# First FFN of an encoder block: four pairs of w1/w3 feature tiles by seven half-size products

## The chip, the cores and the metric

The kernel runs on one core of one Trainium2 chip. The metric is the device time of one execution in microseconds; the time of a kernel is the median of its runs. Engines are named as in the profile: PE (TensorE matmuls), PEld (its weight loads), DVE (VectorE), ACT (ScalarE), POOL (GpSimd), SP (the queue that issues most loads).

## The reference

One layer of an encoder block over x of 512 tokens by 1024 features, in float32:

```python
x = x + 0.5 * swiglu(rms_norm(x, ffn1_norm), ffn1_w1, ffn1_w3, ffn1_w2)     # first FFN
h = rms_norm(x, mix_norm); p = h @ w_in                                     # two mixers and gates
x = x + (gate_a * y_a + gate_b * y_b) @ w_out
x = x + 0.5 * swiglu(rms_norm(x, ffn2_norm), ffn2_w1, ffn2_w3, ffn2_w2)     # second FFN
out = rms_norm(x, final_norm)

def swiglu(h, w1, w3, w2):
    return (jax.nn.silu(h @ w1) * (h @ w3)) @ w2
```

w1 and w3 are 1024 x 2816, w2 is 2816 x 1024. The change touches only the two products with w1 and w3 in the first FFN, and what they need.

## The kernel before

Everything is held with features on the 128 partitions and the 512 tokens along the free side: x is eight tiles `xT[c]` (128 x 512). A matmul takes a 128 x 128 weight tile as the stationary side and streams 512 token columns. Each float32 product is made of three matmuls of a reduced-width type (`mm3`): operands are split into a high part (a cast) and a low part (the rest), and high x high, high x low and low x high are added up in PSUM.

The 2816 hidden features are 22 tiles, j = 0 to 21. For each j the loop in `ffn` loads a 1024 x 128 slice of w1 and one of w3 (512 KB each, `load_raw`, three buffers of tag `raw`, issued on SP's queue), splits it (`split_w`: cast on ACT into `whi`, subtraction on DVE into `wlo`, two buffers each), and `nrm.cols` runs 8 k-tiles x 3 = 24 matmuls into one PSUM bank, `pa` for w1 and `pb` for w3. The x that goes in is scaled by the norm's gain but not yet by the tokens' 1/rms: `rstd` comes out of a sum over all features only during j = 1, so `hidden` multiplies both results by `rstd` on DVE (`fa`, `fb`), takes Silu on ACT, multiplies (`fh`) and splits the hidden tile for w2 (`hh`, `hl`). Tile 0 and the reading and transposing of x are interleaved by hand at the start, with each engine's order fixed by a chain (`Queued`). All else is ordered by a scheduler at compile time: it places an instruction on its engine when its inputs are ready and its buffers free, earlier in the program first. `tc.issue_after(...)` holds an instruction behind a given one on the same engine.

After the 22 tiles, `ffn` multiplies by w2 (`pd`, m = 0 to 7, 22 k-tiles each, loaded in three pieces), adds to `xT[m]`, and `mix_add` parks x and prepares the next norm. `during` is a list of side jobs at given j: `load_params` (2) and `masks` (4) and `place_params` (10), which transposes a block of parameters on PE and casts some small weights on POOL. PSUM is eight banks in three pools: `pm` 2, `pr` 3, `pf` 3.

Of the kernel before, what the change touches and what calls it, by code (L numbers as in the profile page):

```python
# [18 lines left out]
P = 128  # L19
T = 512  # L20
D = 1024
KD = D // P
DFF = 2816
KF = DFF // P
# [26 lines left out]
def kernel(  # L51
# [22 lines left out]
    def tmp(name, shape=(P, T), dt=F32, tag="t", **kw):  # L74
        return tp.tile(list(shape), dt, tag=tag, name=name, **kw)
# [30 lines left out]
    def load_raw(aps, kt, n):  # L106
        raw = wp.tile([P, kt, n], F32, tag="raw", name="raw", bufs=3)
        for c0, src in aps:
            loads.append(nc.sync.dma_start(raw[:, :, c0:c0 + src.shape[1]],
                                           src.rearrange("(k p) c -> p k c", p=P)))  # L110
        return raw

    def split_w(raw, kt, n, eng=None, hi_eng=None):
        hi = wp.tile([P, kt, n], F32R, tag="whi", name="whi", bufs=2)
        lo = wp.tile([P, kt, n], F32R, tag="wlo", name="wlo", bufs=2)
        (hi_eng or act).copy(hi[:], raw[:])  # L116
        (eng or dve).tensor_tensor(lo[:], raw[:], hi[:].bitcast(F32), op=ALU.subtract)  # L117
        return hi, lo
# [4 lines left out]
    def mm3(ps, whi, wlo, xhi, xlo, first, last):  # L123
        pe.matmul(ps, whi, xhi, start=first, stop=False)  # L124
        pe.matmul(ps, whi, xlo, start=False, stop=False)  # L125
        return pe.matmul(ps, wlo, xhi, start=False, stop=last)  # L126
# [14 lines left out]
    def split(dst_hi, dst_lo, src, hi_eng="act"):  # L141
        cast = act.copy(dst_hi, src) if hi_eng == "act" else dve.tensor_copy(dst_hi, src)
        dve.tensor_tensor(dst_lo, src, dst_hi.bitcast(F32), op=ALU.subtract)
        return cast
# [4 lines left out]

    xctx = ExitStack()  # L150
    rtp = xctx.enter_context(tc.tile_pool(name="xr1", bufs=1, side="right"))
    xT = [rtp.tile([P, T], F32, name=f"xT{c}") for c in range(KD)]

    class Norm:

# [32 lines left out]
        def add(s, c):  # L188
            s.scale(c)
            s.square(c)  # L190
# [28 lines left out]
    def pc(i):  # L219
        return par[:, i:i + 1]  # L220
# [24 lines left out]
    with tc.tile_pool(name="x0", bufs=1) as x0:  # L245
# [21 lines left out]
                qpe.transpose(xps[c][:, b * P:(b + 1) * P], xin[c][:, b, :], ident[:])  # L267

        def x_hi(c):
            nrm.hi[c] = xp.tile([P, T], F32R, tag=f"xh{c}", name=f"xh{c}")  # L270
            from_ = (xps if c < 2 else xT)[c][:]
            if c % 2:
                qact.activation(nrm.hi[c][:], from_, AF.Copy, scale=pc(PAR_FFN1 + c))
            else:
                qdve.tensor_scalar(nrm.hi[c][:], from_, pc(PAR_FFN1 + c), None, op0=ALU.mult)

        def x_lo(c):
            nrm.lo[c] = xp.tile([P, T], F32R, tag=f"xl{c}", name=f"xl{c}")
# [154 lines left out]
    def place_params():  # L433
# [9 lines left out]
        pool.tensor_copy(ux[q1], loraw[q1, :])  # L443
        pool.tensor_tensor(ux[q1], loraw[q1, :], f32(ux[q1]), op=ALU.subtract)

    def ffn(nrm, w1, w3, w2, nxt, during=(), first=None, final=None):
        with tc.tile_pool(name="hp", bufs=1) as hp:
            hh, hl = [], []
            def hidden(j, pa, pb):
# [7 lines left out]
                dve.tensor_tensor(h[:], b[:], sa[:], op=ALU.mult)  # L457
                hi = hp.tile([P, T], F32R, name=f"hh{j}")
                lo = hp.tile([P, T], F32R, name=f"hl{j}")
                split(hi[:], lo[:], h[:], "dve")  # L460
                hh.append(hi)
                hl.append(lo)

            summed = None
            for j in range(KF):
# [21 lines left out]
                hidden(j, pa, pb)  # L487
# [12 lines left out]
            if final:  # L500
                final[1](hh, hl, held)
# [713 lines left out]
```

## Time and profile before

| | |
|---|---|
| median of 3 runs | 1189.98 us (1189.31 to 1190.92) |
| the profiled execution | 1189.68 us, of which the span of instructions is 1188.0 us |
| granted TensorE clock | 0.997 of full |
| PE, DVE, ACT, POOL busy | 1173.7, 657.1, 459.3, 87.4 us |
| bytes moved by DMA | 122.52 MB |

How to read it: the profile is of one execution. The span runs from the first to the last instruction; 1.7 us of the execution lie around it. A row of the timeline is start, duration, engine, line, operation and output <- input; a row of the groups adds a count, busy time, mean duration in ns, and the idle time ahead of it with what ended it. A matmul's duration includes the time in which its results drain, so successive matmuls overlap: the distance between starts is what one costs.

### The profile page before, as it was taken

How to read it: one execution, taken by the hardware profiler on the slowest of the kernel's cores; microseconds unless marked ns; L12 is line 12 of the kernel's file. 1: busy time of each engine (PE TensorE's matmuls, PEld its weight loads, DVE VectorE, ACT ScalarE, POOL GpSimd, SP SyncE). 2: the span in 40 equal slices, each digit the busy share in tenths (PEclk: the TensorE clock that was granted, in tenths of full speed). 3: DMA queues.
4: the chain of work that ended last, by engine and by line, in shares of the span. 5: the costliest groups of instructions: out<-in, count | busy, mean ns of one | idle time of the engine just before them, and what ended most of it. 6: DMA issues, size and time to landing. Idle time of an engine off the chain costs nothing.

```text
span 1188.0 us, 15711 instructions
## 1 busy us (share of the span) xinstructions
PE 1173.7 (99%) x6264; PEld 946.0 (80%) x6264; DVE 657.1 (55%) x983; ACT 459.3 (39%) x746; POOL 87.4 (7%) x138
## 2 busy tenths in 40 slices
PE   9999999999999999999999999999999999999997
PEld 7888888888887888887777776778888888888886
DVE  6645554533434697786767656766545454534221
ACT  6322222222223764346786765424222222223222
POOL 1200000001111111411000020121000000000100
PEclk9999999999999999999999999999999999999999
DMA  6333333333334243344122243633333333325211
GB/s 179 111 106 90 106 89 106 89 93 104 114 116 112 78 120 112 109 140 116 37 64 88 81 132 115 211 92 97 89 106 89 103 93 105 91 87 161 89 36 71
DMA packets 201783, 122.52 MB, mean 103 GB/s; under 512 B 9934, under 2 KB 191246, under 8 KB 201710
## 3 DMA queue, kind: packets, MB, share of 16 engines
q1 hardware_dynamic: 195134, 107.62, 31.1%
q0 software_dynamic: 3760, 12.06, 3.2%
q10 hardware_dynamic: 2816, 1.84, 0.5%
q8 instruction: 49, 0.80, 0.3%
q14 instruction: 24, 0.20, 0.1%
HBM read 110.82 MB, written 10.68 MB: 102 GB/s over the span
## 4 chain that ended last, share of the span: by engine, by line
PE 92%; DVE 3%; ACT 3%; DMA 1%; issue 1%; SPq 0%; ACTq 0%; DVEq 0%
PE pb L126 7%; PE pa L126 7%; PE pa L125 7%; PE pb L125 7%; PE pb L124 7%; PE pa L124 7%; PE pd L126 5%; PE pd L124 5%; PE pd L125 5%; PE pgt L124 3%; PE pgt L125 2%; PE pgt L126 2%; PE pk L124 2%; PE pk L125 2%; PE pk L126 2%; PE po L124 2%
## 5 line engine op out<-in xcount | busy, mean ns | idle before, releaser
L116 ACT CAST whi<-raw 128x1024 fp32r<-128x1024 f32 (+3 forms) x193 | 192.7, 999 | 592.0 <-PE pa L125 177.8
L117 DVE TENSOR_TENSOR wlo<-raw,whi 128x1024 fp32r<-128x1024 f32 (+3 forms) x193 | 224.3, 1162 | 125.1 <-ACT whi L116 125.0
L126 PE MATMUL pb<-xh,wlo 128*128 128x512 f32 x344 | 133.9, 389 | 0.0
L126 PE MATMUL pa<-xh,wlo 128*128 128x512 f32 x344 | 133.9, 389 | 0.0
L125 PE MATMUL pa<-xl,whi 128*128 128x512 f32 x344 | 133.9, 389 | 0.0
L124 PE MATMUL pb<-xh,whi 128*128 128x512 f32 x344 | 133.9, 389 | 0.0
L125 PE MATMUL pb<-xl,whi 128*128 128x512 f32 x344 | 133.9, 389 | 0.0
L124 PE MATMUL pa<-xh,whi 128*128 128x512 f32 x344 | 133.9, 389 | 0.0
L455 DVE TENSOR_TENSOR fb<-pb,rstd 128x512 f32<-128x512 f32 x43 | 29.7, 691 | 139.5 <-PE pb L126 139.5
L126 PE MATMUL pd<-hh,wlo 128*128 128x512 f32 x264 | 104.6, 396 | 0.0
L125 PE MATMUL pd<-hl,whi 128*128 128x512 f32 x264 | 104.2, 395 | 0.0
L124 PE MATMUL pd<-hh,whi 128*128 128x512 f32 x264 | 104.2, 395 | 0.0
L126 PEld LDWEIGHTS pb<-xh,wlo 128*128 128x128 f32 x344 | 64.5, 188 | 13.7 <-DVE wlo L241 0.5
L125 PEld LDWEIGHTS pb<-xl,whi 128*128 128x128 f32 x344 | 64.6, 188 | 13.5
L124 PEld LDWEIGHTS pb<-xh,whi 128*128 128x128 f32 x344 | 64.6, 188 | 13.5
L126 PEld LDWEIGHTS pa<-xh,wlo 128*128 128x128 f32 x344 | 64.6, 188 | 13.4
L125 PEld LDWEIGHTS pa<-xl,whi 128*128 128x128 f32 x344 | 64.5, 188 | 13.5
L124 PEld LDWEIGHTS pa<-xh,whi 128*128 128x128 f32 x344 | 64.6, 188 | 13.4
L451 DVE TENSOR_TENSOR fa<-pa,rstd 128x512 f32<-128x512 f32 x43 | 29.7, 691 | 70.2 <-PE pa L126 70.2
L126 PEld LDWEIGHTS pd<-hh,wlo 128*128 128x128 f32 x264 | 49.6, 188 | 12.3 <-DVE wlo L117 0.5
L125 PEld LDWEIGHTS pd<-hl,whi 128*128 128x128 f32 x264 | 49.6, 188 | 11.9
L124 PEld LDWEIGHTS pd<-hh,whi 128*128 128x128 f32 x264 | 49.6, 188 | 11.8
(397 smaller groups left out, 2031.1 us busy)
## 6 DMA issues: line engine op xcount, KB each, us to landing
raw<-in_ffn_w_dram SPq DMA_DIRECT2D x121, 512.0 KB
raw<-in_w_in_dram SPq DMA_DIRECT2D x40, 512.0 KB
raw<-in_ffn_w_dram SPq DMA_DIRECT2D x12, 384.0 KB
raw<-in_w_out_dram SPq DMA_DIRECT2D x8, 512.0 KB
gsave<-gs SPq DMA_DIRECT2D x9, 256.0 KB
xin<-in_x_dram SPq DMA_DIRECT2D x8, 256.0 KB
xsave<-xT POOLq DMA_DIRECT2D x8, 256.0 KB, 2.3
G<-gsave POOLq DMA_DIRECT2D x8, 256.0 KB, 3.0
```

The source lines that it names most:

```text
L116: (hi_eng or act).copy(hi[:], raw[:])
L117: (eng or dve).tensor_tensor(lo[:], raw[:], hi[:].bitcast(F32), op=ALU.subtract)
L124: pe.matmul(ps, whi, xhi, start=first, stop=False)
L125: pe.matmul(ps, whi, xlo, start=False, stop=False)
L126: return pe.matmul(ps, wlo, xhi, start=False, stop=last)
L451: dve.tensor_tensor(a[:], pa[:], nrm.rstd[:], op=ALU.mult)
L455: dve.tensor_tensor(b[:], pb[:], nrm.rstd[:], op=ALU.mult)
```

## The change

For j = 6 to 13 the loop takes two feature tiles at a time (`wino`, four times: `NW, W0 = 4, 6`). The product of a pair is seen as blocks of two by two: weights by feature tile (j or j+1) and half of the 1024 inputs, tokens by half of the inputs and half of the 512 tokens. A scheme of the Strassen family makes the four result blocks out of seven products of blocks instead of eight, with sums of blocks on both sides. A product is 24 matmuls of 256 columns: w1 and w3, four k-tiles, three terms.

- The scheme needs x already normalized. `renorm` multiplies `xT` in place by gain and `rstd` (after j = 2 and 3 of the program) and splits it again into `B`. The raw x is written to memory first (`xkeep`, by POOL) and read back on SP's queue after the last j.
- `token_sums` (after j = 4 and 5) makes four sums of token blocks, split into `TB`.
- Three buffers of 8 KB a partition (tag `R`) hold x at first, the token sums, and then in turn the weight blocks of the pairs: r for the first half of the inputs (a11, a21) and r for the second (a12, a22), 1 MB each, loaded as 256 columns of w1 and w3.
- Of the four weight sums two are made on DVE (`s1`, and s1 + a11 in the place of a11), and two by transfers that POOL issues and that add to their target (`onto`): A11 onto a21, and A12 onto a11. Each `onto` is two transfers of 256 KB with rows of 512 B.
- Each of the seven weight blocks is split into high and low parts (`w_parts`); two splits in three go to the buffers of `whi` and `wlo`, the third into two of the three `raw` buffers.
- The products are p11, p2, p1, p12, p3, p4, p22, in this order on PE; seven additions or subtractions of 512 elements on DVE and one copy on ACT combine them. From j = 6 on `hidden_n` needs no `rstd`.
- For j > 1 of the first FFN the cast of the hidden tile moves from DVE to ACT; `place_params` moves from j = 10 to j = 16; the split x of the start moves to a pool `hx` whose tiles later hold hidden tiles 6 to 13.

The diff, cut to its core:

```diff
-    xT = [rtp.tile([P, T], F32, name=f"xT{c}") for c in range(KD)]
+    def place(shape, name, dt=F32):
+        return rtp.tile([P, *shape], dt, tag="R", name=name, bufs=3)
+    xr = [place((KD // 2, T), f"xr{i}") for i in range(2)]
+    xT = [xr[c // 4][:, c % 4] for c in range(KD)]
+    xkeep = dp.tile([KD, P, T], F32, name="xkeep")
...
+        for i in range(2):
+            nc.gpsimd.dma_start(xkeep[4 * i:4 * i + 4].rearrange("c p t -> p c t"), xr[i][:])
...
+            def renorm(cs):
+                for c in cs:
+                    dve.scalar_tensor_tensor(xT[c], xT[c], pc(nrm.gain + c), nrm.rstd[:], op0=ALU.mult, op1=ALU.mult)
+                    hi = xp.tile([P, T], F32R, tag=f"xh{c}", name=f"xn{c}")
+                    lo = xp.tile([P, T], F32R, tag=f"xl{c}", name=f"xm{c}")
+                    split(hi[:], lo[:], xT[c])
+                    B.append((hi, lo))
...
+            def token_sums(n):
+                l, r = slice(0, HT), slice(HT, T)
+                if n == 0:
+                    TB.append(place((2, HK, HT), "tsum"))
+                D = TB[0]
+                if n == 0:
+                    dve.tensor_tensor(D[:, 0], xr[0][:, :, r], xr[0][:, :, l], op=ALU.subtract)
+                    t_parts(0, D[:, 0])
+                    dve.tensor_tensor(D[:, 1], xr[1][:, :, r], xr[0][:, :, r], op=ALU.subtract)
+                    t_parts(1, D[:, 1])
+                else:
+                    dve.tensor_tensor(D[:, 0], xr[1][:, :, r], D[:, 0], op=ALU.subtract)
+                    t_parts(2, D[:, 0])
+                    dve.tensor_tensor(D[:, 1], D[:, 0], xr[1][:, :, l], op=ALU.subtract)
+                    t_parts(3, D[:, 1])
...
+            def w_parts(src):
+                n = count[0] % 3
+                count[0] += 1
+                hi = wp.tile([P, KD, P], F32R, tag="raw" if n == 2 else "whi", name="ah", bufs=3 if n == 2 else 2)
+                lo = wp.tile([P, KD, P], F32R, tag="raw" if n == 2 else "wlo", name="al", bufs=3 if n == 2 else 2)
+                split(hi[:], lo[:], src)
+                return hi, lo
+            def wino(j):
+                cs = slice(j * P, (j + 2) * P)
+                A = []
+                for h in range(2):
+                    r = place((2 * HK, 2 * P), "aw")
+                    for i, w in enumerate((w1, w3)):
+                        loads.append(nc.sync.dma_start(
+                            r[:, i * HK:(i + 1) * HK],
+                            w[0][h * HK * P:(h + 1) * HK * P, cs].rearrange("(k p) c -> p k c", p=P)))
+                    A.append((r[:, :, 0:P], r[:, :, P:2 * P]))
+                (a11, a21), (a12, a22) = A
+                p11 = w_parts(a11)
+                s1 = wp.tile([P, KD, P], F32, tag="raw", name="asum", bufs=3)
+                add = lambda o, x_, y_: dve.tensor_tensor(o, x_, y_, op=ALU.add)
+                add(s1[:], a22, a21)
+                def onto(dst, k0, c):
+                    for i, w in enumerate((w1, w3)):
+                        pool.dma_start(dst[:, i * HK:(i + 1) * HK],
+                                       w[0][k0 * P:(k0 + HK) * P, c * P:(c + 1) * P].rearrange("(k p) c -> p k c", p=P),
+                                       accum_op=ALU.add)
+                onto(a21, 0, j)
+                add(a11, s1[:], a11)
+                p2 = w_parts(a11)
+                p1 = w_parts(s1[:])
+                p12 = w_parts(a12)
+                onto(a11, HK, j)
+                p3 = w_parts(a21)
+                p4 = w_parts(a11)
+                p22 = w_parts(a22)
...
+                def product(name, pool_, parts, block):
+                    ps = pool_.tile([P, 2, HT], F32, tag="b", name=name)
+                    hi, lo = parts
+                    for i in range(2):
+                        for k, (bh, bl) in enumerate(block):
+                            q = i * HK + k
+                            mm3(ps[:, i], hi[:, q], lo[:, q], bh, bl, k == 0, k == HK - 1)
+                    return ps
...
+                pa = product("wa", pm, p11, x_block(0, 0))
+                t1 = half_tmp("t1")
+                act.copy(t1[:], pa[:])
+                pb = product("wb", pr, p2, t_block(2))
+                u2 = half_tmp("u2")
+                dve.tensor_tensor(u2[:], pb[:], t1[:], op=ALU.subtract)
...
+            ready = {2: lambda: renorm(range(0, HK)), 3: lambda: renorm(range(HK, KD)),
+                     4: lambda: token_sums(0), 5: lambda: token_sums(1)}
...
+                if first and j in ready:
+                    ready[j]()
+                j += 1
+            if first:
+                xr[:] = [place((KD // 2, T), f"xb{i}") for i in range(2)]
+                for i in range(2):
+                    loads.append(nc.sync.dma_start(xr[i][:], xkeep[4 * i:4 * i + 4].rearrange("c p t -> p c t")))
...
-    ffn(nrm, ffn1_w1, ffn1_w3, ffn1_w2, mix_add, {2: load_params, 4: masks, 10: place_params}, (first, second))
+    ffn(nrm, ffn1_w1, ffn1_w3, ffn1_w2, mix_add, {2: load_params, 4: masks, 16: place_params}, (first, second))
```

More of the change, by code (lines that the diff above doesn't have):

```diff
@@ L269, in x_hi @@
         def x_hi(c):
-            nrm.hi[c] = xp.tile([P, T], F32R, tag=f"xh{c}", name=f"xh{c}")
+            pair = hx.tile([P, 2, T], F32R, tag=f"h{6 + c}", name=f"px{c}")
+            nrm.hi[c], nrm.lo[c] = pair[:, 0], pair[:, 1]
             from_ = (xps if c < 2 else xT)[c][:]
@@ L277, in x_lo @@
         def x_lo(c):
-            nrm.lo[c] = xp.tile([P, T], F32R, tag=f"xl{c}", name=f"xl{c}")
             from_ = (xps if c < 2 else xT)[c][:]
@@ L448, in ffn, with hidden_parts @@
             hh, hl = [], []
+            def hidden_parts(j, h):
+                if first and W0 <= j < W0 + KD:
+                    t = hx.tile([P, 2, T], F32R, tag=f"h{j}", name=f"hid{j}")
+                else:
+                    t = hp.tile([P, 2, T], F32R, tag=f"h{j}", name=f"hid{j}")
+                split(t[:, 0], t[:, 1], h, "act" if first and j > 1 else "dve")
+                hh.append(t[:, 0])
+                hl.append(t[:, 1])
             def hidden(j, pa, pb):
@@ L457, in hidden, with hidden_n @@
                 dve.tensor_tensor(h[:], b[:], sa[:], op=ALU.mult)
[L458 to L462, printed above, removed]
-            summed = None
-            for j in range(KF):
+                hidden_parts(j, h[:])
+            def hidden_n(j, a, b, sa, h):
+                act.activation(sa, a, AF.Silu)
+                dve.tensor_tensor(h, b, sa, op=ALU.mult)
+                hidden_parts(j, h)
@@ new lines, in ffn @@
+            summed = None
+            j, normed_ = 0, False
+            ready = {2: lambda: renorm(range(0, HK)), 3: lambda: renorm(range(HK, KD)),
+                     4: lambda: token_sums(0), 5: lambda: token_sums(1)}
+            while j < KF:
+                if first and W0 <= j < W0 + 2 * NW:
+                    if not normed_:
+                        nrm.hi, nrm.lo = [h for h, l in B], [l for h, l in B]
+                        normed_ = True
+                    wino(j)
+                    j += 2
+                    continue
@@ L486, in ffn @@
                         during[j]()
-                hidden(j, pa, pb)
+                if normed_:
+                    sa, h = tmp("fs"), tmp("fh")
+                    hidden_n(j, pa[:], pb[:], sa[:], h[:])
+                else:
+                    hidden(j, pa, pb)
+                if first and j in ready:
+                    ready[j]()
+                j += 1
+            if first:
+                xr[:] = [place((KD // 2, T), f"xb{i}") for i in range(2)]
+                for i in range(2):
+                    loads.append(nc.sync.dma_start(xr[i][:], xkeep[4 * i:4 * i + 4].rearrange("c p t -> p c t")))
+                xT[:] = [xr[c // 4][:, c % 4] for c in range(KD)]
             cuts = ((0, 8), (8, 8), (16, 6))
```

35 lines of the change are left out of this document (added).

## The prediction

> **What bounds the kernel now.** I read first the page's busy times and the shares of its chain of waits.
>
> ```profile
> span 1188.0 us, 15711 instructions
> PE 1173.7 (99%) x6264; PEld 946.0 (80%) x6264; DVE 657.1 (55%) x983; ACT 459.3 (39%) x746; POOL 87.4 (7%) x138
> PE 92%; DVE 3%; ACT 3%; DMA 1%; issue 1%; SPq 0%; ACTq 0%; DVEq 0%
> ```
>
> The second line is busy time and share by engine, the third the share of the chain that ended last. TensorE is 99% busy and 92% of the chain: time taken off its stream comes off the kernel, unless something else then holds it up. So the next view is the stretch that the change rewrites. In order of time, feature tile 6 (the first that the change pairs) starts at 77.06 us and tile 14 at 164.25 us; below are these two starts, the matmul before the first, and the busy table of this stretch and of the one ahead of it (columns: stretch, length, PE, PEld, DVE, ACT, POOL with counts, clock, DMA share, GB/s).
>
> ```profile
> 76.83 0.39 PE L126 MATMUL pb<-xh,wlo 128*128 128x512 f32 x1
> 77.06 0.39 PE L124 MATMUL pa<-xh,whi 128*128 128x512 f32 x1
> 164.25 0.39 PE L124 MATMUL pa<-xh,whi 128*128 128x512 f32 x1
> 31.00:77.00 46.00, 46.00 (x204) 38.09 (x204) 26.75 (x34) 13.01 (x15) 6.12 (x7) 1.00 0.39 114
> 77.06:164.25 87.19, 87.19 (x387) 72.14 (x385) 43.90 (x58) 21.61 (x24) 0.00 (x0) 1.00 0.33 97
> ```
>
> Eight feature tiles x 2 weight matrices x 8 k-tiles x 3 terms = 384 matmuls fill 87.19 us without a hole (the three others are a transpose and the edges): 0.227 us each, at full clock. VectorE is half idle there (43.90 of 87.19), ScalarE three quarters. The groups of that stretch give the price of one:
>
> ```profile
> L124 PE MATMUL pb<-xh,whi 128*128 128x512 f32 x64 | 24.9, 389 | 0.0
> L117 DVE TENSOR_TENSOR wlo<-raw,whi 128x1024 fp32r<-128x1024 f32 x16 | 19.6, 1222 | 1.3 <-ACT whi L116 1.3
> L116 ACT CAST whi<-raw 128x1024 fp32r<-128x1024 f32 x16 | 16.9, 1054 | 65.6 <-PE pa L125 34.9 <-PE pb L125 30.7
> L126 PEld LDWEIGHTS pa<-xh,wlo 128*128 128x128 f32 x64 | 12.0, 188 | 2.6
> L457 DVE TENSOR_TENSOR fh<-fb,fs 128x512 f32<-128x512 f32 x8 | 5.5, 692 | 0.7
> ```
>
> ScalarE's 65.6 us before `whi` end on matmuls: the splits wait for a free `whi`, not for data. The weights come early and TensorE never waits for them.
>
> **The change part by part.**
>
> *TensorE.* Four pairs of tiles now take 7 products each; a product is 2 matrices x 4 k-tiles x 3 terms = 24 matmuls of 256 columns. So 4 x 168 = 672 half matmuls replace 384 whole ones, each with its own weight load. Everything hangs on the spacing of 256-column matmuls. The trace has some in the attention logits (L978, L979); two places in order of time, and their group:
>
> ```profile
> 571.17 0.19 PEld L978 LDWEIGHTS lp<-kb,qa 128*128 128x128 f32 x1 [0.65 <-ACT qrn L818]
> 571.28 0.19 PEld L979 LDWEIGHTS lp<-klc,qb 128*128 128x128 f32 x1
> ...
> 571.70 0.28 PE L979 MATMUL lp<-klc,qb 128*128 128x256 f32 x1
> 571.82 0.23 PE L980 MATMUL lp<-dmask,identb 128*128 128x128 bf16 x1
> ...
> 574.39 0.27 PE L979 MATMUL lp<-klc,qb 128*128 128x256 f32 x1
> 574.50 0.23 PE L980 MATMUL lp<-dmask,identb 128*128 128x128 bf16 x1
> L979 PE MATMUL lp<-klc,qb 128*128 128x256 f32 x8 | 2.2, 279 | 0.0
> ```
>
> After a 256-column matmul the next starts 0.12 and 0.11 us later. Two weight loads follow each other in 0.11 us, so loads (188 ns each, but overlapping) do not quite set the pace. I take 0.120 us: 672 x 0.120 = 80.6 us against 384 x 0.227 = 87.1, a gain of **6.5 us**. The rows lie one matmul deep, not in a stream; as bounds I take 0.117 (78.6 us, gain 8.5) and 0.123 (82.7 us, gain 4.4). The pair becomes 168 x 0.12 = 20.2 us, a product 2.9 us.
>
> The Trainium skill, "TensorE: Matmul & The Clock Gate", section "Back-to-back issue gap", gives N/2.4 + 2.5 ns for an isolated gap, an estimate of 109 ns at 256 columns. By it the sum would be 73 us. The trace disagrees at 512 columns already: 227 ns against its 216.
>
> *VectorE and ScalarE in the pairs.* Each product needs its weights split (cast 1.05, subtract 1.22), seven a pair where there were four; two block sums run on VectorE (1.22 each); seven combinations of 512 elements out of PSUM and four operations for the two hidden tiles (0.69 each). In one tile before, VectorE and the queue of loads look so:
>
> ```profile
> 78.06 0.69 DVE L457 TENSOR_TENSOR fh<-fb,fs 128x512 f32<-128x512 f32 x1
> 78.67 1.22 DVE L117 TENSOR_TENSOR wlo<-raw,whi 128x1024 fp32r<-128x1024 f32 x1
> 79.80 0.42 DVE L142 CAST hh<-fh 128x512 fp32r<-128x512 f32 x1
> 79.91 16.15 SPq L109 DMA_DIRECT2D raw<-in_ffn_w_dram  x4
> ```
>
> Start to start these are 0.61 (78.06 to 78.67) and 1.13 (78.67 to 79.80). VectorE: 9 x 1.13 + 11 x 0.61 = 16.9 us of a 20.2 us pair (by durations 9 x 1.22 + 11 x 0.69 = 18.6). ScalarE: 7 x 1.05 + about 5 x 0.6 = 10.4. VectorE goes from half to over four fifths full: no bound by itself, but whatever needs it will queue.
>
> *The loop from pair to pair.* The weight blocks sit in three buffers, and a pair uses two. So the second block of the next pair (a12, a22) can be fetched only once p3 and p4 of this pair are split, and p4 is the last to come. Round the loop: load; s1 = a22 + a21 (1.22); the sum onto a11 (1.22); split of p2 (1.05 + 1.22); the adding transfers onto a11; split of p4 (1.05 + 1.22). The load is 1 MB; half of it can be read off the transfer rows:
>
> ```profile
> 81.00:82.00 1.00, 1.00 (x6) 0.84 (x5) 0.00 (x0) 0.00 (x0) 0.00 (x0) 1.00 0.70 202
> 82.00:83.00 1.00, 1.00 (x6) 0.81 (x6) 0.30 (x1) 0.53 (x1) 0.00 (x0) 1.00 1.02 309
> xsave<-xT POOLq DMA_DIRECT2D x8, 256.0 KB, 2.3
> Tall<-Td POOLq DMA_DIRECT2D x2, 128.0 KB, 5.8
> 439.46 1.38 POOL L725 DMA_DIRECT2D Ld<-G  x2 [0.96 <-DVE G L717]
> ```
>
> A 512 KB tile issued at 79.91 flows from 81 to 83 at up to 309 GB/s, so 1 MB takes about 1.1 + 1024 KB / 309 = 4.5, say 5.0 us. No transfer of this kernel adds to its target. Two plain ones of 256 KB issued by GpSimd cost 0.69 (half of 1.38) + 2.3 = 3.0 us at least; two of the slowest kind here 2 x 5.8 = 11.6. I take 6, twice the plain cost, because each byte is also read from the target; both ends stay for the range. The loop is then 5.0 + 1.22 + 1.22 + 2.27 + 6 + 2.27 = 18.0, with seven hand-overs at 0.1 us (an estimate; above, the subtraction ends at 79.89 and the load that waits for it issues at 79.91, but a chain between engines is slower) 18.7, against 20.2: it just fits.
>
> The new waits stand in queues. Behind an adding transfer GpSimd has only the next one; behind a block load SP has only later loads; but behind the cast for p3 or p4, if its transfer is late, ScalarE has the Silu and the casts of the next products, and VectorE behind their subtractions the combinations that empty PSUM. Each product writes one of eight banks, so TensorE notices after some three products, 8 us.
>
> p4 also waits for its split buffers, free when the third product ends. Counted from the start S of a pair: 8.6 + 0.2 + 2.3 = 11.1, load 16.1, s1 17.3, sum 18.5, p2 split 20.8; its product is due at 20.2 + 2.9 = 23.1. That leaves 2.3 us, while VectorE in the same stretch has the last combinations and hidden tiles of the old pair to do (about eight of 0.61). I charge 0.5 us at each of three hand-overs: **1.5 us lost**.
>
> *The way in.* Tiles 2 to 5 carry the renormalizing (8 multiplications, 8 subtractions) and the token sums (4 additions, 4 subtractions of 1024), and x is parked in memory first.
>
> ```profile
> 16.31 0.75 DVE L241 SCALAR_TENSOR_TENSOR xl<-xT,par,xh 128x512 fp32r<-128x512 f32 x1
> 17.82 0.59 ACT L241 COPY xT<-xtp 128x512 f32<-128x512 f32 x1 [0.72 <-PE xtp L241]
> 30.07 0.63 ACT L207 ACTIVATE rstd<-rln 128x512 f32<-128x512 f32 x1
> 30.46 0.71 POOL L438 CAST uw<-loraw 32x512 fp32r<-32x512 f32 x1 [25.85 <-DMA loraw<-in_rwkv_w_up_dram]
> xS<-xsave POOLq DMA_DIRECT2D x8, 256.0 KB, 7.1
> ```
>
> x is whole at 18.4 us and 2 MB of parking takes some 9 (the eight `xS` transfers), so it is ready when rstd is, at 30.7. GpSimd's cast of place_params ran at 30.46, from tile 10 of the program: work is moved up to where it is ready, and the sums should be too. They cost 8 x 0.67 (0.75 less the overlap of 0.08 seen above) + 8 x 0.61 + 8 x 1.13 = 19.3 us start to start; between 31 and 77 VectorE has 46.0 - 26.8 = 19.2 us free, and 2 to 4 more, since durations overlap by 0.08 and tiles 2 to 4 lose a cast. Both buffers of x are then free about 8 us before 77.06, two thirds of the work having sufficed for the first. With a 5 us load and 4.9 us to the split of p2, due at 80, that is just in time: **nothing charged**, with little cover. If it is late, TensorE waits for it one for one.
>
> *The rest.* x is loaded back (2 MB, some 8 us of transfers) on SP's queue between the last w1/w3 and the first w2 tile. Loads there run about four groups (20 us) ahead: hidden. Tiles 14 to 21 lose two multiplications each on VectorE, and place_params moves from tile 10 to 16; neither is on the path.
>
> Sum on the profiled execution, 1189.68 us (span 1188.0 and 1.7 around it): - 6.5 + 1.5 = **1184.7**. The median shown, 1189.98, is 0.3 higher; I give 1184.8.
>
> **The rivals.**
>
> *The loop sets the pace (slower).* If the adding transfers take X, the loop is 12.7 + X, and with about 1.5 us of queueing on VectorE 14.2 + X. From X = 6 on it is longer than a pair, and three rounds pay the excess. At X = 9: 23.2, three times 3.0 less the gain of 6.5 is + 2.5 us, 1192; at X = 11.6: 25.8, 3 x 5.6 - 6.5 = + 10, 1200. For it: nothing in the trace adds on transfer, 512 B rows, three buffers for four pairs. Against: 256 KB moved in 2.3 us.
>
> *The way in is late (slower).* Left at their place in the program, the last token sums start behind tile 5's hidden product, at 81; the buffer is free at 83.4, loaded at 88.4, p2 split at 93.3 instead of 80: 13 us, + 7, so 1197. Against: the cast at 30.46.
>
> *VectorE is the bound (same).* By durations it has 18.6 us a pair; with 0.15 us of hand-over for each of 20 operations that is 21.6, and 87.19 / 4 = 21.8 was the time before: about 1189.
>
> *Loads do not hide behind short matmuls (much slower).* Then each costs its 188 ns: 672 x 0.188 = 126 us, 1229. Against: the 0.12 and 0.11 above. The Trainium skill, "TensorE: Matmul & The Clock Gate", section "The mechanism", lets a weight load overlap a running matmul only when the row group differs, which would do this. The trace denies it: at 512 columns matmul and load together take 227 ns, of which the load alone would be 188.
>
> *Short matmuls are cheaper than I take.* 389 - 279 = 110 ns for 256 columns; a spacing of that would give 73.9 us, 1176.5.
>
> **How the numbers follow.** Forecast 0.50; loop 0.22; way in 0.12; VectorE 0.10; loads 0.03; cheaper matmuls 0.03. About 0.2% (2.4 us) is what a measurement of this kernel can tell from no change. Faster: 0.50 + 0.03 = 0.53. Same: VectorE 0.10 and a mild loop 0.04 = 0.14. Slower: 0.18 + 0.12 + 0.03 = 0.33. The forecast's own range is 1181.3 (0.117 and no waits) to 1187. The whole range is 1181.3 to 1199: it leaves out the loads, the cheaper matmuls and the worst tenth of loop and way in.
>
> **What would show it.** Right: half matmuls about 0.12 us apart; 672 of them in about 82 us; VectorE 85 to 92% busy there; waits of TensorE short and ahead of p2. Wrong: a first wait of many us before the first or second product of pair 6 (way in); waits before p2, p3 or p4 of every later pair that trace back to the adding transfers (loop); a spacing near 0.19 (loads). The adding transfer's time from issue to landing is the number I know least.

## The result, and the profile after

The kernel with the change takes 1206.5 us (median of 4 runs, 1205.2 to 1208.4), the kernel before beside it 1190.1 (1189.3 to 1190.9): slower, ratio 1.0139, 95% interval 1.0121 to 1.0156. The prediction of 1184.8 and its range up to 1199 both missed. First the changed kernel's busy times and the shares of its chain of waits, as on the page:

```profile
span 1203.4 us, 16412 instructions
PE 1176.0 (98%) x6552; PEld 959.3 (80%) x6552; DVE 686.6 (57%) x1003; ACT 490.9 (41%) x794; POOL 115.1 (10%) x156
PE 84%; DVE 6%; DMA 4%; ACT 3%; issue 2%; POOL 0%; SPq 0%; ACTq 0%; DVEq 0%; POOLq 0%
```

TensorE had 92% of the chain before and has 84% now; VectorE and DMA have taken the difference. TensorE is busy 2.3 us longer although its stream got shorter, and the span is 15.4 us longer. Where that arises is read from starts in the timeline: the matmul before the first pair and the pair's first, three half matmuls in the middle of a pair, the first matmul of tile 14, and then the busy table (columns as in the prediction) of the way in and of the pairs.

```profile
84.75 0.39 PE L126 MATMUL pb<-px,wlo 128*128 128x512 f32 x1
84.98 0.28 PE L124 MATMUL wa<-xn,ah 128*128 128x256 f32 x1
...
89.98 0.28 PE L124 MATMUL wc<-th,ah 128*128 128x256 f32 x1
90.10 0.28 PE L125 MATMUL wc<-tl,ah 128*128 128x256 f32 x1
90.22 0.28 PE L126 MATMUL wb<-th,al 128*128 128x256 f32 x1
...
176.46 0.40 PE L124 MATMUL pa<-xn,whi 128*128 128x512 f32 x1
31.00:85.00 54.00, 49.41 (x206) 39.04 (x205) 48.15 (x57) 23.54 (x32) 10.51 (x9) 0.97 0.48 129
84.98:176.46 91.48, 84.37 (x671) 83.32 (x670) 65.17 (x77) 37.58 (x46) 17.97 (x14) 0.96 0.64 139
```

Undisturbed half matmuls start 0.12 us apart, as forecast. But the first pair starts at 84.98 instead of 77.06 (7.9 us late), and the four pairs last 91.48 us instead of 87.19 (4.3 more; at 0.1195 us each, 672 matmuls would fill 80.3, so 11.2 us are lost in them). Tile 14 is thus 12.2 us late. Another 0.5 is lost in tiles 14 to 21, and 3.0 us appear some 600 us later, at the products with `rwkv_proj` (57.0 us before, 60.0 after, by the starts of their first matmul and of the first one of `w_out`). Together that is 15.7; the rest of the kernel is 0.3 us shorter. Now the three places.

**The way in.** Waits of the weight loads from 31 to 85 us (engine, tile, line, who released it: us in all, times, longest), then VectorE's rows and one of GpSimd's casts beside them, and TensorE's first long wait:

```profile
PEld pb L126 <- DVE wlo L117: 3.6, 1, 3.6
PEld pb L124 <- ACT whi L116: 1.4, 1, 1.4
30.28 0.69 DVE L473 TENSOR_TENSOR fa<-f,rstd 128x512 f32<-128x512 f32 x1
30.89 7.15 DVE L495 SCALAR_TENSOR_TENSOR xr<-xr,par,rstd 128x512 f32<-128x512 f32 x8
37.96 0.68 DVE L477 TENSOR_TENSOR fb<-f,rstd 128x512 f32<-128x512 f32 x1
38.56 2.87 DVE L143 TENSOR_TENSOR xm<-xr,xn 128x512 fp32r<-128x512 f32 x2
42.49 1.21 DVE L117 TENSOR_TENSOR wlo<-raw,whi 128x1024 fp32r<-128x1024 f32 x1
33.48 0.96 POOL L449 CAST uw<-loraw 32x512 fp32r<-32x512 f32 x1
43.76 0.50 PE L126 MATMUL pb<-px,wlo 128*128 128x512 f32 x1 [3.21 <-DVE wlo L117]
```

All eight multiplications of `renorm` stand between `fa` and `fb` of tile 0, 7.15 us in one block, and more of the preparation ahead of tile 2's second weight split (`wlo`, 42.49). TensorE waits for that split until 43.76. The eight also take 0.89 us each; what runs beside them is GpSimd's casting (five casts and two subtractions of `place_params`, from 32.67 to 40.87 us). After TensorE's wait of 3.2 us the granted clock is 0.64 from 43.70 to 48.50 us.

**The pairs.** The waits of the weight loads from 75 to 182 us, ScalarE's longest, and the rows of ScalarE, SP, VectorE and TensorE around the second pair's first product, with the `asum` of the next two pairs and the busy table right after the wait:

```profile
PEld wa L126 <- DVE al L143: 3.8, 1, 3.8
PEld we L124 <- ACT ah L142: 2.2, 1, 2.2
ACT ah L142 <- DMA aw<-in_ffn_w_dram: 15.2, 4, 6.5
94.32 2.99 ACT L142 CAST ah<-aw 128x1024 fp32r<-128x1024 f32 x3 [4.58 <-DMA aw<-in_ffn_w_dram]
97.14 1.22 DVE L143 TENSOR_TENSOR al<-aw,ah 128x1024 fp32r<-128x1024 f32 x1
98.38 2.71 SPq L539 DMA_DIRECT2D aw<-in_ffn_w_dram  x4
104.66 1.23 DVE L546 TENSOR_TENSOR asum<-aw 128x1024 f32<-128x1024 f32 x1 [4.57 <-issue]
107.60 1.22 DVE L143 TENSOR_TENSOR al<-aw,ah 128x1024 fp32r<-128x1024 f32 x1
108.87 0.39 PE L126 MATMUL wa<-xn,al 128*128 128x256 f32 x1 [3.60 <-DVE al L143]
109.93 1.22 DVE L546 TENSOR_TENSOR aw<-asum,aw 128x1024 f32<-128x1024 f32 x1
129.74 1.23 DVE L546 TENSOR_TENSOR asum<-aw 128x1024 f32<-128x1024 f32 x1 [1.15 <-DMA aw<-in_ffn_w_dram]
149.63 1.23 DVE L546 TENSOR_TENSOR asum<-aw 128x1024 f32<-128x1024 f32 x1 [0.67 <-DMA aw<-in_ffn_w_dram]
109.00:113.50 4.50, 4.50 (x26) 4.50 (x27) 4.50 (x7) 2.83 (x5) 0.00 (x0) 0.62 0.77 96
```

ScalarE stands four times in front of a cast that needs an adding transfer, 15.2 us in all. Behind the first of these waits (94.32) stand the casts of p4, p3 and p22 together: p4's is the one that waits, p3's data had landed 20 us before. Only when p4 and p3 are split (97.14, until 98.36) is the buffer of the next pair's second block free, and its load is issued (98.38; the row also holds the first block of the third pair, from 100.12). Only with that load can `asum` run (104.66); the trace names no releaser for this wait, but the data flow at 319 to 374 GB/s from 100 to 105 us, and the next two `asum` wait for such a load by name. Behind `asum`, in VectorE's order, stand three combinations of the old pair and the split of the next pair's p11 (107.60), whose cast ended at 103.04. TensorE waits for that split. The last row gives what the wait costs beyond itself: in the 4.5 us after it the granted clock is 0.62 and 26 half matmuls run where about 38 would. The Trainium skill, "TensorE: Matmul & The Clock Gate", section "What's actually happening", says that after an idle window of about 3.4 us the clock is halved until a busy one has passed; the trace agrees here (after this wait of 3.6 us most starts are 0.213 apart for some 3.4 us, then 0.12 again).

**Far away.** ScalarE's and TensorE's waits around 745 to 785 us, before and after, and the transfers that read x back for `w_out`:

```profile
ACT whi L116 <- DMA raw<-in_rwkv_proj_dram: 2.8, 1, 2.8
PE ppj L124 <- ACT whi L116: 1.0, 1, 1.0
```

```profile
ACT whi L116 <- DMA raw<-in_rwkv_proj_dram: 4.2, 1, 4.2
PE ppj L124 <- ACT whi L116: 2.4, 1, 2.4
xS<-xsave POOLq DMA_DIRECT2D x8, 256.0 KB, 7.7
```

A wait of 1.0 us has become 2.4, with a lower clock behind it (0.79 from 768 to 776 us); the weights that are late were loaded beside the `xS` transfers, whose landing went from 7.1 us to 7.7.

### The profile page after: what moved, and what is told of

It reads as the page before. It is cut to its first block, busy times and chain, and to the rows that moved or that the text cites. A ratio compares the mean times of both kernels' runs of the same rounds, so it can differ in the third digit from the quotient of the medians.

```text
span 1203.4 us, 16412 instructions
## 1 busy us (share of the span) xinstructions
PE 1176.0 (98%) x6552; PEld 959.3 (80%) x6552; DVE 686.6 (57%) x1003; ACT 490.9 (41%) x794; POOL 115.1 (10%) x156
## 4 chain that ended last, share of the span: by engine, by line
PE 84%; DVE 6%; DMA 4%; ACT 3%; issue 2%; POOL 0%; SPq 0%; ACTq 0%; DVEq 0%; POOLq 0%
PE pb L124 5%; PE pb L126 5%; PE pb L125 5%; PE pd L124 5%; PE pd L125 5%; PE pd L126 5%; PE pa L126 5%; PE pa L124 5%; PE pa L125 5%; DMA aw<-in_ffn_w_dram 3%; PE pgt L124 3%; PE pgt L125 2%; PE pgt L126 2%; PE pk L124 2%; PE pk L125 2%
## 5 line engine op out<-in xcount | busy, mean ns | idle before, releaser
L116 ACT CAST whi<-raw 128x1024 fp32r<-128x1024 f32 (+2 forms) x177 | 175.7, 994 | 508.4 <-PE pd L125 132.4
L117 DVE TENSOR_TENSOR wlo<-raw,whi 128x1024 fp32r<-128x1024 f32 (+2 forms) x177 | 203.7, 1151 | 151.7 <-ACT whi L116 150.9
L126 PE MATMUL pd<-hid,wlo 128*128 128x512 f32 x264 | 104.5, 396 | 0.0
L124 PE MATMUL pd<-hid,whi 128*128 128x512 f32 x264 | 104.2, 395 | 0.0
L125 PE MATMUL pd<-hid,whi 128*128 128x512 f32 x264 | 104.2, 395 | 0.0
L125 PE MATMUL pb<-xl,whi 128*128 128x512 f32 x176 | 68.5, 389 | 0.0
L124 PE MATMUL pb<-xh,whi 128*128 128x512 f32 x176 | 68.5, 389 | 0.0
L125 PE MATMUL pa<-xl,whi 128*128 128x512 f32 x176 | 68.5, 389 | 0.0
L124 PE MATMUL pa<-xh,whi 128*128 128x512 f32 x176 | 68.5, 389 | 0.0
L126 PE MATMUL pa<-xh,wlo 128*128 128x512 f32 x176 | 68.5, 389 | 0.0
L125 PEld LDWEIGHTS pd<-hid,whi 128*128 128x128 f32 x264 | 49.6, 188 | 12.0
L124 PEld LDWEIGHTS pd<-hid,whi 128*128 128x128 f32 x264 | 49.6, 188 | 11.9
L142 ACT CAST ah<-aw 128x1024 fp32r<-128x1024 f32 x24 | 24.7, 1046 | 35.2 <-DMA aw<-in_ffn_w_dram 15.2
```

## The experiments

Times are medians beside runs of the kernel before on the same chip; where no ratio stands, there is one time of that kernel and no interval.

**e1: preparation without pairs.** `renorm`, `token_sums` and `xkeep` stay; tiles 6 to 13 are computed one by one with the normalized x.

```diff
-                if first and W0 <= j < W0 + 2 * NW:
...
-                    wino(j)
-                    j += 2
-                    continue
+                if first and j == W0:
+                    nrm.hi, nrm.lo = [h for h, l in B], [l for h, l in B]
+                    normed_ = True
```

> Everything of the change but the pairs: x is parked, normalized in place, the token sums are made and split, x is read back; tiles 6 to 13 run as ordinary tiles with 512 columns on the normalized x. Theory A (the way in): VectorE gets all of this ahead of the weight splits of tiles 2 and 3, and TensorE starves there. In the changed kernel tile 4 starts at 62.4 us where it started at 55.3, and the tiles up to the first pair lose 0.8 more, so this kernel should lose the same 7 to 8 us: 1197 to 1199, with TensorE's holes between 38 and 52 us. Rival (what fills VectorE and ScalarE there is the early work of the first pair, its casts and sums): 1190 to 1192 and no hole.

Measured: 1199.4, ratio 1.0079 (1.0064 to 1.0094). Tile 6 starts at 85.18, and the waits of the way in are the same. So the way in alone costs about 8 of the 9.4 us, and the pairs come on top.

**e2: the preparation in small steps.** Twelve steps (eight tiles of x, four sums), each held behind an operation of tiles 1 to 5 on VectorE, so that they cannot be moved ahead of these tiles' own work.

```diff
+            def some(n, behind):
+                with tc.issue_after(behind.ins):
+                    for _ in range(n):
+                        if prep:
+                            prep.pop(0)()
...
+                got = dve.tensor_tensor(a[:], pa[:], nrm.rstd[:], op=ALU.mult)
+                if first and 2 <= j:
+                    some(2, got)
```

> The same work as the change; only the preparation is cut into 12 steps (one x tile, or one token sum), each held behind an operation of tiles 1 to 5 on VectorE, two steps at a time. Theory A: the holes of 38 to 52 us go, tile 4 starts before 57 us and the first pair at 78 to 80 instead of 85; with the waits inside the pairs unchanged the time is 1199 to 1202. Rival (the first pair's blocks are free later, so the pair waits for what tiles 2 and 3 no longer wait for): no gain, 1205 to 1209, with the wait now ahead of the first products of the first pair.

Measured: 1203.7, ratio 1.0116 (1.01 to 1.0131); the first pair at 80.53. Some 4.5 us of the way in went, less than expected, and the pairs lost part of it again (93.7 us). One row says what was left in the way: a cast on VectorE that takes 0.42 us elsewhere and ran here while GpSimd cast:

```profile
40.87 1.51 DVE L142 CAST hid<-fh 128x512 fp32r<-128x512 f32 x1
```

**e3: a buffer of its own for the block (a12, a22).** Still three buffers, but this block always takes the same one.

```diff
-        return rtp.tile([P, *shape], dt, tag="R", name=name, bufs=3)
+        return rtp.tile([P, *shape], dt, tag="R1" if one else "R2", name=name, bufs=1 if one else 2)
...
-                    r = place((2 * HK, 2 * P), "aw")
+                    r = place((2 * HK, 2 * P), "aw", one=h == 1)
```

> Only the three block buffers are shared out otherwise: the block of a12 and a22 always takes the buffer of the last pair's a12 and a22, which is free once p12 and p22 are split and s1 is made; so its load no longer waits for the adding transfers and the split of p4. Theory B (the loop from pair to pair: load, s1, sum, split of p2, adding transfers, split of p4, load): the waits at the first product of pair 1 (3.9 us and a lower clock behind it) and at p2 of pair 2 go, 5 to 7 us less in all, 1199 to 1202. Rival (not the buffer but VectorE's and ScalarE's order is late: instructions that wait for transfers stand ahead of ready ones): the loads come earlier but the waits stay within 2 us of what they were, 1204 to 1208.

Measured: 1209.5, ratio 1.0173 (1.0156 to 1.019): worse, and the theory as I had put it fell. ScalarE's wait and the table of the pairs in this kernel:

```profile
ACT ah L142 <- DMA aw<-in_ffn_w_dram: 17.0, 4, 7.1
85.54:180.22 94.68, 84.44 (x671) 82.89 (x670) 65.97 (x76) 37.31 (x46) 17.98 (x14) 0.96 0.60 126
```

With the buffer of its own the load waits for another reader, p22. That one needs no transfer, but its cast stood on ScalarE behind those of p4 and p3, which do; its split ended at 100.95, and the load was issued at 100.97, behind that of the third pair's first block (99.24). Counted from the start of the first pair that is 15.4 us, where the change had 13.4.

**e4: the transfers overwrite instead of adding.** Same transfers, same bytes; two of the four sums are then not formed.

```diff
-                                       accum_op=ALU.add)
+                                       )
```

> The four transfers a pair that GpSimd issues onto a21 and a11 no longer add, they overwrite (the sums are not formed: two of the seven products have wrong weights); size, rows and order are the same. It prices the adding. In the change two of them take 2.6 us to issue, 4.9 us from issue to landing (median) and some 6 to 7.6 from source ready to split. If adding costs a second pass over the target, as I took it (6 against 3.0 us): landing falls to 2.5 to 3.5 us and the kernel to 1198 to 1203. Rival (the cost is in GpSimd writing 512 descriptors for rows of 512 B): landing stays at 4 to 5 us, the kernel within 2 us of the change.

Measured: 1199.6. Landing and ScalarE's wait:

```profile
aw<-in_ffn_w_dram POOLq DMA_DIRECT2D x16, 256.0 KB, 3.5
ACT ah L142 <- DMA aw<-in_ffn_w_dram: 5.7, 2, 3.0
```

Landing was 4.9 with adding: adding costs 1.4 us a transfer, and the four pairs last 85.0 instead of 91.5 us. Of the weight loads' waits the one of 3.8 us is still there (3.6); the others inside the pairs are gone, and with that before `we` the lower clock behind it. Transfers as short as plain ones thus cover much of the loss, but not the second pair's first product.

**e5: p22 ahead of the adding transfer.** e3's buffers, and p22 is split and multiplied before p3 and p4, so that nothing without need of a transfer stands behind one.

```diff
+                p22 = w_parts(a22)
                 onto(a11, HK, j)
                 p3 = w_parts(a21)
                 p4 = w_parts(a11)
-                p22 = w_parts(a22)
...
+                pb = product("wf", pr, p22, t_block(3))
+                dve.tensor_tensor(u2[:], u2[:], pb[:], op=ALU.subtract)
                 pb = product("wd", pr, p3, t_block(1))
```

> The buffers shared out as in the run with own buffers, and p22 split and multiplied ahead of p3 and p4 (the combinations changed to fit; the same sums). Theory C, formed from the last runs: the casts for p3 and p4 wait up to 7 us for the adding transfers and stand in ScalarE's queue ahead of p22's cast; the end of p22's split frees the block buffer, so the load of the next pair waited for the transfers whichever buffer it took. Now nothing that frees the second block's buffer stands behind a transfer, and p3 and p4 are due 3 and 6 us later: from the first whole product of pair 0 to tile 14 it should take 82 to 85 us instead of 91.5, the kernel 1197 to 1200. Rival (VectorE, 85 to 90% full in the pairs, is what is late): 89 us or more, 1203 or more.

Measured: 1198.1, ratio 1.0066 (1.005 to 1.0081).

```profile
ACT ah L142 <- DMA aw<-in_ffn_w_dram: 5.0, 2, 2.8
PEld wa L126 <- DVE al L143: 2.3, 1, 2.3
86.99:169.74 82.75, 80.41 (x671) 79.99 (x670) 65.24 (x76) 36.25 (x44) 17.98 (x14) 1.00 0.69 148
```

With the same adding transfers (landing 5.2), the pairs fall to 82.75 us, 4.4 less than the eight tiles took before, at full clock; the load is issued 11.7 us after the start of the first pair. So transfers of this length can be hidden, and against e3 the order alone makes the difference (94.68 to 82.75). Two things remain together here: the order frees the buffer earlier, and it lets p3 and p4 be due one product later. The order without e3's buffers was not run. The way in is as late as before (first pair at 86.99), and the kernel is still slower.

**e6: all four weight sums on VectorE, no adding transfers.**

```diff
-                onto(a21, 0, j)
+                add(a21, a21, a11)
...
-                onto(a11, HK, j)
+                add(a11, a11, a12)
```

> The four block sums of a pair all on VectorE, no adding transfers; buffers and order as in the change. If the transfers' time in the loop is what holds the pairs (theory C), the two added sums (2 x 1.13 us a pair, VectorE then 19.2 of 20.2) cost less than the 6 to 7 us they replace: pairs 86 to 89 us instead of 91.5, kernel 1200 to 1203. Rival (VectorE's fill decides): pairs 93 us or more, kernel above 1207.

Measured: 1203.7, pairs 91.3 us. That lies between the two expectations and settles nothing by itself (the order is that of the change): the waits are many and small (the largest 3.4 before `wc`), spread over casts and splits.

**e7: e5 and e2 together, GpSimd's casts held behind the last adding transfer.**

```diff
+        with tc.issue_after(onto_last[-1].ins):
+            params_pool()
```

> The new order and buffers, the preparation in steps held behind tiles 1 to 5, and GpSimd's casts of the small weights (place_params) held behind the last adding transfer: in the run with steps VectorE's operations took 1.1 to 1.8 us instead of 0.7 while these casts ran (37 to 42 us). Theory A and C together: the hole ahead of tile 4 shrinks to 0 to 1 us (tile 4 at 55.5 to 56.5), the pairs take 82 to 85 us: 1187 to 1192. Rival (the steps delay the pair's blocks, which own buffers and order do not mend): the first pair waits, 1195 or more.

Measured: 1189.3 against 1190.1, ratio 0.9989 (0.998 to 0.9998). First pair 77.93, pairs 81.4 us, tile 14 at 159.36, which is 4.9 us ahead of before. Of these only 0.5 arrive at the end: TensorE still waits 2.4 us for `rwkv_proj`, and more is lost in the mixers' stretch between 370 and 710 us, whose length varies by 1.5 us from kernel to kernel here without a pattern that I could find.

**e8: before, shifted by 128 bytes.** In e7 tiles 1 to 5 still ran at 0.232 us a matmul instead of 0.227, as in the changed kernel. The only difference in their data is where the streamed x lies: in slots of `hx`, byte 160 of a 256-byte line, while `xh` and `xl` lie at byte 32, as the weights do. In the kernel before, hidden tiles lie at 160 too, and `pd` runs at 0.233. The places are those of the allocation; the profiles hold no addresses.

```diff
             hh, hl = [], []
+            hp.tile([P, 32], F32, name="shift")
```

> The kernel before, with an unused tile of 128 bytes a partition ahead of the hidden tiles; nothing else differs. Seen so far: matmuls of 512 columns are 0.2267 us apart when the streamed tile lies in the slots of xh and xl, and 0.232 to 0.234 apart when it lies in those of the hidden tiles, before and after alike; since the change keeps the x of tiles 1 to 5 in the latter, these run at 0.2323. In the allocation the former (and the weight tiles whi, wlo) start at byte 32 of a 256-byte line, the latter at byte 160. Theory P (the place within 256 bytes sets the spacing): with the shift the hidden tiles start at byte 32 too, the 528 matmuls of w2 in each FFN fall from 0.2333 to 0.227, pd from 123.2 to about 119.8 us, and the kernel gains 3.4 us in the first FFN and 1 to 3.4 in the second: 1183 to 1186. Rival (the region of the memory, or what lies in the tile, sets it): 0.2333 as before, 1190.

Measured: 1184.6 against 1190.4, ratio 0.9953 (0.9938 to 0.9968). Rows of `pd`, before and then shifted:

```profile
300.05 0.39 PE L126 MATMUL pd<-hh,wlo 128*128 128x512 f32 x1
300.28 0.40 PE L124 MATMUL pd<-hh,whi 128*128 128x512 f32 x1
300.51 0.39 PE L125 MATMUL pd<-hl,whi 128*128 128x512 f32 x1
300.74 0.40 PE L126 MATMUL pd<-hh,wlo 128*128 128x512 f32 x1
300.98 0.39 PE L124 MATMUL pd<-hh,whi 128*128 128x512 f32 x1
```

```profile
300.15 0.39 PE L124 MATMUL pd<-hh,whi 128*128 128x512 f32 x1
300.38 0.39 PE L125 MATMUL pd<-hl,whi 128*128 128x512 f32 x1
300.61 0.39 PE L126 MATMUL pd<-hh,wlo 128*128 128x512 f32 x1
300.83 0.39 PE L124 MATMUL pd<-hh,whi 128*128 128x512 f32 x1
301.06 0.39 PE L125 MATMUL pd<-hl,whi 128*128 128x512 f32 x1
```

Four steps take 0.93 us in the first and 0.91 in the second; over the stage, `pd` falls from 123.2 to 119.7 us. The edit moves nothing but the hidden tiles. By the profiles 3.5 us come in the first FFN's `pd` and 1.3 in the second's; the rest of the 5.8 is not traced.

**e9: e7, shifted by 1920 bytes** (tiles of x in `hx` too).

```diff
     hx = hctx.enter_context(tc.tile_pool(name="hx", bufs=1))
+    hx.tile([P, 480], F32, name="shift")
...
+            if not first:
+                hp.tile([P, 480], F32, name="shift2")
```

> The kernel of e7 with an unused tile of 1920 bytes a partition ahead of the hidden tiles (and of the x of tiles 1 to 5): they then lie like the weight tiles within 256 and within 2048 bytes. Theory P: tiles 1 to 5 at 0.227 instead of 0.2323 (1.3 us less before the first pair, which starts at about 76.7), pd 3.4 less, second FFN 1 to 3.4 less: 1181 to 1184 where e7 had 1189.3. If the shift of 128 does nothing and this one does, the place within 2048 bytes counts, not that within 256. Rival (region or content): no change, 1189.3.

Measured: 1182.4, ratio 0.9933 (0.9916 to 0.995). First pair at 76.60, 0.5 ahead of the kernel before; `pd` 119.7 us. Shifts of 128 and of 1920 bytes both work: of the places that I compared, the one within 256 bytes is what they have in common.

**e10: e9, and x for `w_out` read back by SP, in twos behind the loads of `rwkv_proj`.**

```diff
-        for c in range(KD):
-            nc.gpsimd.dma_start(xT[c][:], xsave[c])
...
+            if 2 <= m < 6:
+                with tc.issue_after(loads[-1].ins):
+                    for c in (2 * m - 4, 2 * m - 3):
+                        nc.sync.dma_start(xT[c][:], xsave[c])
```

> As e9, and the eight transfers that read x back ahead of w_out are no longer issued by GpSimd all at once, but by SP in twos behind the rwkv_proj loads of four tiles. Theory (the late rwkv_proj load stands beside these transfers): the wait of TensorE in the rwkv_proj products, 2.6 us in the pair kernels and 1.0 before, falls under 0.5, and the kernel is 1.5 to 3 us faster than e9. Rival (that load is late for a reason of its own): the wait stays and the time is that of e9 within 0.5; or x comes too late for w_out and it is slower.

Measured: 1179.3, ratio 0.9907 (0.9892 to 0.9922). TensorE's longest wait between 700 and 800 us, and the pairs:

```profile
PE pw L124 <- ACT whi L116: 0.5, 2, 0.3
76.59:159.48 82.89, 81.15 (x673) 80.74 (x672) 67.81 (x77) 37.21 (x45) 29.86 (x23) 1.00 0.74 155
```

No wait for `rwkv_proj` is left, though the same bytes move at about the same time (issued from 736.1 to 744.0 us, in e9 from 736.6 to 741.4). So the far-away 3 us came from these transfers as GpSimd issued them, all at once; whether the queue or the spreading in twos helps was not told apart, and why they land later in the kernels with pairs stays open.

**e11: the change as it was, with GpSimd's casts alone held back** (the edit of e7).

> The kernel after with one difference: the casts that GpSimd does for place_params (some 8 us, at 32 to 41 us) are held behind the last adding transfer. Theory (half of the late way in is VectorE slowed by GpSimd's casts): the renormalizing operations run at their usual 0.67 to 0.75 us, the holes of TensorE between 40 and 55 us shrink by 2 to 4 us, the first pair starts at 81 to 83 instead of 85.0, and the kernel takes 1202.5 to 1204.5. Rival (the order on VectorE alone makes the holes): first pair at 84 to 85, 1205.5 to 1206.5.

Measured: 1201.2, against 1206.5. VectorE's block, and the wait that was 3.6 us:

```profile
31.17 5.38 DVE L501 SCALAR_TENSOR_TENSOR xr<-xr,par,rstd 128x512 f32<-128x512 f32 x8
PEld pb L126 <- DVE wlo L117: 0.3, 1, 0.3
```

The same eight multiplications take 5.38 us instead of 7.15 (0.67 each instead of 0.89), the wait of 3.6 us falls to 0.3, and the first pair starts at 80.76: 4.2 of the 7.9 us came from GpSimd at work beside VectorE, more than expected. The Trainium skill, "SBUF — State Buffer", section "SBUF: two separate sides", says that VectorE operations with two inputs in this memory and GpSimd operations that read it hold a shared port one at a time. The trace agrees in direction. A cast of one input (1.51 us in e2) was slowed as well; no run here shows by what.

**e12: before, with the shift of e8 and the transfers of e10: the control.**

> The kernel before with the shift of 128 bytes of e8 and the later reading back of x of e10, but without the change: the control for e10 (1179.3), which holds both and the pairs. If the pairs themselves gain what their stretch shows in e10 (tile 14 of the program starts 4.8 us earlier than before, of which about 0.4 come from tiles 1 to 5 starting earlier or running alike), this kernel takes about 1179.3 + 4 = 1183, and the wait of 1.0 us in the rwkv_proj products goes. If the two side changes bring all of it, this kernel takes about 1179 too.

Measured: 1183.6, ratio 0.9937 (0.9923 to 0.9951). The pairs, well ordered, are thus worth 1183.6 - 1179.3 = 4.3 us, which is what their stretch shows (82.89 against 87.19). The two ran on different chips and with different shifts (128 and 1920 bytes); by their ratios it is 3.6 us.

## Why the prediction was wrong, by its own steps

- **TensorE's stream: right.** 0.120 us was taken, 0.119 to 0.120 measured; at this spacing alone the gain would be 6.9 us where 6.5 was forecast. The rival "loads do not hide" fell, and with it the rule of the Trainium skill that the prediction names beside it: half matmuls run at 0.12 with a weight load of 0.19 each. "Cheaper matmuls" and "VectorE is the bound" fell too (VectorE is 71% busy in the pairs, 82% in e10, not 85 to 92).
- **The way in, "nothing charged": the step that failed first, 7.9 us.** I argued that the scheduler moves work up to where it is ready, so the sums would come early, and took VectorE's free time from 31 to 77 us as room. It did move them up, but ahead of splits that TensorE needed at once. Free time on average is not free time in front of a due split. The causes overlap: the order alone gains 4.5 us (e2), GpSimd's casts alone 4.2 (e11), both 7.1 (e7, where the pairs have e5's order too), and the place of the streamed x 1.3 more (e7 to e9). My rival "the way in is late" named the place and nearly the size (1197; e1 has 1199.4) with the opposite mechanism, sums that come too late; that the size agrees is luck.
- **The loop, "1.5 us lost": 11.2 us lost.** The step that failed is "I charge 0.5 us at each of three hand-overs". The prediction counted from the start S of a pair; for the first pair S is 84.98. The load was forecast at S + 11.1 and came at S + 13.4, because p4's cast waited for its transfer until S + 9.3 and p3's split stood behind p4's. `asum` was forecast to end at 17.3 and ended at 20.9, because the load took 6.3 us and not 5, beside the 1 MB of the third pair's first block. The sum onto a11 was forecast at 18.5 and ended at 26.2, because VectorE did six other operations between the two sums (from 105.81 to 109.93). Five of them are combinations and a multiplication of the old pair; I had written "about eight of 0.61", which is 4.9 us, beside a slack of 2.3, and still charged 0.5. The sixth, the split of the next pair's p11, was not in the list at all: it stood behind `asum`, and TensorE waited 3.6 us for it. Eight banks did not cover this: they hold results, and what ran out was the next weights. From `asum` to `asum` the second and third round took 25.1 and 19.9 us, where I had 18.7. e3 shows that another buffer alone does not mend this, e5 that buffer and order together do with the transfers as they are, and e4 that shorter transfers hide most of it. The rival "loop sets the pace" had the place, but its price, the transfers' time X, was only part of it.
- **The adding transfers: 6 us, right by luck.** From the first of two issues to the cast that waits they took 6.2 to 7.9. The 6 was twice a plain cost of 3.0; e4 has 4.2 for two plain ones (0.74 to the second issue and 3.5 to its landing), and adding makes them about one and a half times as long, not twice.
- **The clock was not in the sum.** Behind the wait of 3.6 us in the second pair 18 half matmuls took 3.66 us (from 109.09) where 2.15 would do, behind that of 2.0 us before `we` 17 took 3.53 (from 167.24): 1.5 us more each, and the wait of 3.2 us on the way in has the same behind it. A wait of 2.3 us in e5 has not: its pairs show a clock of 1.00. So the length of one wait alone does not decide it here.
- **x read back: right.** No wait stands before the first w2 product.
- **Not seen at all: 3 us at `rwkv_proj`.** Before the change ScalarE already waited 2.8 us for a load there and TensorE 1.0, some 500 us behind the last line that I costed; I took the rest of the kernel as fixed.

## What to carry to other kernels

A step that waits on an in-order queue costs what stands behind it, not its own length: list the followers of each new wait, and put whatever needs nothing ahead of it. Work that is "free" on a half-idle engine must be given its places by hand, in pieces as short as the gaps, and not beside an engine that slows it. And a matmul's spacing that is a few per cent off its best in one stage and not in another is worth a comparison of addresses: here a padding of 128 bytes gained more (5.8 us) than the whole scheme of seven products (4.3).

## What the runs showed of the hardware that I had not expected

- 512-column matmuls are 0.227 us apart with the streamed tile at byte 32 of 256 by the allocation, like the weights, and 0.232 to 0.234 at byte 160 (`pd`: 119.7 and 123.2 us). Whether it is the place itself or the place relative to the weights was not tried.
- Adding to the target costs a 256 KB transfer 1.4 us (landing 4.9 against 3.5, median), and GpSimd 1.28 us for its issue against 0.74 (17.97 and 10.41 us for 14 of them).
- GpSimd's small casts slowed VectorE by a third (0.89 against 0.67 us), and single operations up to 3.6 times (1.51 against 0.42).
- Eight transfers of 256 KB delayed another queue's loads when GpSimd issued them, and did not when SP issued them two at a time in its own order (wait of 2.6 us in e9, none in e10).
